# Other places, queues and steps for partial sums, x and head outputs in a hybrid attention layer on one core

## The chip, the cores and the metric

The kernel runs on one core of a Trainium2 chip. The metric is the device time of one execution in microseconds; lower is better. The runs shown of the kernel before took 2504.91, 2508.32 and 2502.14 us, median 2504.91.

## What is computed

One decoder layer over 1024 tokens of width 2048, all in float32. x is normalised and multiplied by a weight matrix of 2048 x 8192; the columns are q, k, v and gate of 8 stick-breaking heads and of 8 differential heads (partial rotary on q and k of the latter). Cut to what matters:

```python
hn = rmsnorm(h, norm_mix_g)
sb_q, sb_k, sb_v, sb_g, df_q, df_k, df_v, df_g = split(hn @ w_in)
sb_out = stick_breaking_attention(sb_q, sb_k, sb_v)        # w = sigmoid(z) * prod of (1 - sigmoid)
df_out = rmsnorm(differential_attention(df_q, df_k, df_v, lam), subln_g)
mixed = concat([sb_out * silu(sb_g), df_out * silu(df_g)])
h = h + mixed @ w_out
h = h + sigmoid(rmsnorm(h, norm_ple_g) @ w_ple_gate) * (p @ w_ple_proj)
return rmsnorm(h, norm_final_g)
```

## The kernel before, in words

Everything is kept transposed: features on 128 partitions, tokens along the free axis, in two halves of 512 tokens with the order of the tokens reversed. "Half 1" is worked on first and "half 0" second (for brevity: the first half and the second half of the attention stage). Every float32 operand is split into a rounded part and a rest (hi and lo, fp32r), and a product of two operands is three matmuls: hi x hi, lo x hi, hi x lo (L219 to L221 in `unit`, L517 to L519 in `Seven.product`). ScalarE (ACT) makes the hi part, VectorE (DVE) the lo part.

The order of the work: (1) v and gate of the stick-breaking heads for both halves by a seven-product scheme of 2 x 2 blocks (class `Seven`, instance `gv`, L645 to L943); its results go to the DRAM tile `vg_d`. (2) Attention: for each half, heads 8 to 15 (differential), then 0 to 7 (stick-breaking), L957 to L1060. A differential head has two units of projection, a stick-breaking one has one; a unit is 32 groups of three matmuls. (3) The output projection, again with `Seven` (instance `op`, L1175 to L1357), (4) gate, embedding and final norm.

**Filler and side steps.** TensorE's order is written out by hand (`manual_schedule`). While TensorE does a unit, the attention of the head before is woven in: `attention` returns a list of (slot, function), `Side.add` sorts it behind the current slot, and `Side.tick` is called after each group of three matmuls in `unit` (and in `Seven.product` where `tick` is set) and runs what is due. So a "slot" is one group of three matmuls. Of each head there are `weights` (scores for one block of 128 query rows; matmuls L289 to L298), `values` (transposition of v, L343), and for two pairs of row blocks `turn` (transposition of weights, L359, then hi and lo, L368 to L376) and `mix` (weights times v, L391 to L396; after the last one the sum is read by ACT L401 and DVE L402), and for differential heads `norm` (L422, L423). `SECOND` and `LATD` set when the second pair starts, `tight` marks head 15. The PSUM tiles av, tp, vps, msq and ssps share the tag "t" with two buffers.

**The other queues.** Outside the stretches marked `man2`, VectorE and ScalarE are ordered by a scheduler ahead of the run, as SyncE's (SP) and GpSimd's (POOL) DMA queues are everywhere: it takes what it holds ready, in the order of the program. Each engine then works strictly in that order. SP issues weights (L153, L532, L562), x (L663, L716, L965), operands (L1184) and the stores of L1219; POOL issues the stores of L743 and L698, the loads of vf and gf (L984), of k and v, and the accumulating stores into `comb_d` (L254 to L265).

**First sums.** In both uses of `Seven` the first eight units (phase 0) start with a filler: for each pair of units the product "A11" is made, copied to a tile s1 (tag "sq", two buffers) and stored (`vgpart_d`, L743, or `part_d`, L1219), then "A12" is added and the sum goes out through a tile of the ring "f" (four buffers, `ftile`). After the filler, for each unit, s1 is loaded again (L885, L1298) and added to the product "S2" (L893, L1306) before the product "S1" follows.

**x of the second half.** For half 0 each of 16 blocks of x is loaded into a tile "xt" (four buffers, L965) and split into xh and xl by `split_scaled` (L139, L140). The tiles xh and xl of a block are the ones that the first half used, so they are free when TensorE has read them for the last time. The DRAM tile `h_d`, to which the output projection is added later, gets its copy of x in half 0 (L1060) and, for eight blocks, earlier (L930).

Of the kernel before, what the change touches and what calls it, by code (L numbers as in the profile page):

```python
# [17 lines left out]
ALU = mybir.AluOpType  # L18
# [30 lines left out]
def _body(ctx, nc, tc, ap):  # L49
# [218 lines left out]
    def attention(at, pz, half, hd, q, qz, K, KL, VV, sg, vf):  # L268
# [188 lines left out]
    with tc.tile_pool(name="at", bufs=2) as at, tc.tile_pool(name="pz", bufs=2, space=PSUM) as pz:  # L457
# [23 lines left out]
        class Seven:  # L481

            def __init__(self, w, n):
                self.w = w
                self.units = [(ph, u) for ph in range(2) for u in range(n)]
                self.wq, self.XC, self.T = {}, {}, {}
                self.made, self.late, self.slot = [], 0, 0
                self.raws = []
                self.xq = deque()
                self.after = None  # L490
# [32 lines left out]
            def first(self, u, parts=((slice(0, 2), slice(0, 4 * P)),), between=None):  # L523

                raw = wp.tile([P, 2, 4 * P], F32, name="wraw", tag="wraw", bufs=2)
                self.raws.append(raw)
                hi = wp.tile([P, 2, 4 * P], F32R, name="wfh", tag="whi")
                lo = wp.tile([P, 2, 4 * P], F32R, name="wfl", tag="wlo")
                for k, f in parts:
                    if isinstance(k, slice):  # L530
                        for j in range(2):
                            nc.sync.dma_start(raw[:, j, f], self.w(u, 0, j)[:, 0, f])  # L532
                    else:
                        nc.sync.dma_start(raw[:, k, f], self.w(u, 0, k)[:, 0, f])
                    if between:
                        between(k, f)

                def cast(k, f):
# [3 lines left out]
                for i, nm in enumerate(("A11", "A12")):  # L542
                    self.wq[u, 0, nm] = hi[:, i], lo[:, i]
                if between:
                    return cast
                for k, f in parts:
                    cast(k, f)
# [153 lines left out]
        cast0 = gv.first(0, parts[:2], xloads)  # L701
        cast1 = gv.first(1, parts1, lambda k, f: None)
        for i in range(4):
            load1(1, i)
            if i == 1:
                nc.sync.dma_start(gv.raws[0][:, 1, :], gv.w(0, 0, 1)[:, 0, :])
                nc.sync.dma_start(gv.raws[1][:, 1, :], gv.w(1, 0, 1)[:, 0, :])
# [20 lines left out]
        nslot = 0  # L728
# [6 lines left out]
        for u in range(0, H, 2):  # L735
            aa = [pp.tile([P, HALF], F32, name="pa", tag="acc", bufs=2) for _ in range(2)]
            for i in range(2):
                gv.product(u + i, 0, "A11", aa[i], True)
                s1 = ev.tile([P, HALF], F32, name="s1", tag="sq", bufs=2)
# [4 lines left out]
                if u:  # L744
                    some(4)
            for i in range(2):
# [4 lines left out]
                if u < H - 2:  # L751
                    gv.first(u + 2 + i)
# [117 lines left out]
        for ph in range(2):  # L870
            for u in range(H):
# [5 lines left out]
                s1 = ev.tile([P, HALF], F32, name="s1", tag="sq", bufs=2)  # L877
# [6 lines left out]
                else:  # L884
# [72 lines left out]
        for half in (1, 0):  # L957
# [4 lines left out]
            else:  # L962
                for kt in KT:
                    xt = ev.tile([P, HALF], F32, name="xt", tag="xt", bufs=4)
                    nc.sync.dma_start(xt, ap["xT"][kt * P:(kt + 1) * P, tsl])  # L965
                    X[kt] = split_scaled(kt, xt, gvec[:, 0, kt:kt + 1])
# [3 lines left out]
            for hd in (ORDER0, ORDER1)[half]:  # L970
# [9 lines left out]
                acc = unit(X)  # L980
                if sb:
                    vf, gf = f32t("vf"), f32t("gf")
                    for i, t in enumerate((vf, gf)):
                        G.dma_start(t, vg_d[half, i, hd])  # L984
# [40 lines left out]
                if sb:  # L1025
                    vacc = vf, gf
# [254 lines left out]
        for ph in range(2):  # L1281
            for u in range(8):
# [7 lines left out]
                s1 = ev.tile([P, HALF], F32, name="s1", tag="sq", bufs=2)  # L1290
# [6 lines left out]
                else:  # L1297
# [251 lines left out]
```

## Time and profile before

| what | value |
|---|---|
| median of the runs shown | 2504.91 us |
| the profiled execution's own time | 2504.86 us |
| its span, first to last instruction | 2503.1 us |
| mean granted TensorE clock | 0.989 |
| DMA, mean over the span | 161 GB/s |

In a table of stretches each row gives the stretch in us from the start of the span and its length, then the busy time with the count of instructions for TensorE (PE), its weight loads (PEld), VectorE, ScalarE and GpSimd, then the granted TensorE clock, the busy share of the DMA engines and GB/s. In a timeline each row gives start and duration in us, engine, line, operation, output<-inputs, shapes and count; in brackets stands how long the engine sat idle before it and what ended that. Where the engine named had been done for long, another wait ended last. A "q" behind an engine's name is its queue.

### The profile page before, as it was taken

What the parts mean: (1) busy time and instruction counts of PE and PEld (TensorE: products, weight loads), DVE (VectorE), ACT (ScalarE), POOL (GpSimd) and SP (SyncE); (2) the same over time, 40 slices, a digit from 0 to 9 for tenths busy, and PEclk for the clock granted to TensorE, in tenths of its full rate; (3) what the DMA queues carried; (4) which work ended last, traced back from release to release, by engine and by line L of the source; (5) the groups of instructions that cost most, each with busy time, mean ns of one, the idle gap of its engine ahead of it and who ended that gap; (6) DMA issues with size and microseconds to landing.
All of it is one profiled execution on the core that took longest, in us unless ns stands there. A gap on an engine that the chain in (4) does not pass through costs nothing.

```text
span 2503.1 us, 31940 instructions
## 1 busy us (share of the span) xinstructions
PE 2419.8 (97%) x11434; PEld 2007.0 (80%) x11434; DVE 1793.0 (72%) x3010; ACT 1216.1 (49%) x2066; POOL 297.5 (12%) x393
## 2 busy tenths in 40 slices
PE   8999999999999999999999989999899999999997
PEld 6787878888888887888888877887787887787886
DVE  6888776777777777778888877778578664546555
ACT  6243345555565445555656664445423224546443
POOL 1211110000010010000000001110111112330110
PEclk9999999999999999999999999999999999999998
DMA  8777654434344555444444434545746777343333
GB/s 287 265 261 225 213 185 137 153 118 135 121 143 152 164 170 179 128 125 122 125 128 116 125 110 118 144 126 177 244 160 215 169 189 230 119 133 103 130 110 102
DMA packets 165424, 397.72 MB, mean 159 GB/s; under 512 B 18896, under 2 KB 23248, under 8 KB 165264
## 3 DMA queue, kind: packets, MB, share of 16 engines
q1 hardware_dynamic: 126432, 293.68, 36.6%
q0 software_dynamic: 38832, 102.00, 15.4%
q8 instruction: 90, 1.47, 0.2%
q14 instruction: 70, 0.57, 0.1%
HBM read 297.03 MB, written 106.95 MB: 161 GB/s over the span
## 4 chain that ended last, share of the span: by engine, by line
PE 78%; DVE 8%; issue 7%; DMA 3%; ACT 3%; POOL 1%; SPq 0%; DVEq 0%; POOLq 0%; ACTq 0%
PE acc L219 16%; PE acc L220 16%; PE acc L221 16%; PE pbc L517 3%; PE pbc L519 3%; PE pbc L518 3%; PE tp L359 2%; DVE st L320 1%; PE av L396 1%; PE z L297 1%; PE z L298 1%; PE pa L517 1%; PE pa L519 1%; PE pa L518 1%; PE av L394 1%
## 5 line engine op out<-in xcount | busy, mean ns | idle before, releaser
L219 PE MATMUL acc<-xh,whi 128*128 128x512 f32 x1568 | 629.8, 402 | 1.5 <-DVE gt L1166 1.5
L221 PE MATMUL acc<-xh,wlo 128*128 128x512 f32 x1568 | 614.5, 392 | 0.0
L220 PE MATMUL acc<-xl,whi 128*128 128x512 f32 x1568 | 614.3, 392 | 0.0
L150 DVE TENSOR_TENSOR wlo<-wraw,whi 128x1024 fp32r<-128x1024 f32 x252 | 312.5, 1240 | 240.9 <-ACT whi L149 235.5
L149 ACT CAST whi<-wraw 128x1024 fp32r<-128x1024 f32 x252 | 264.9, 1051 | 290.0 <-PE acc L220 260.2
L221 PEld LDWEIGHTS acc<-xh,wlo 128*128 128x128 f32 x1568 | 295.8, 189 | 64.8 <-DVE wlo L150 0.2
L219 PEld LDWEIGHTS acc<-xh,whi 128*128 128x128 f32 x1568 | 296.3, 189 | 57.2 <-issue 2.4
L220 PEld LDWEIGHTS acc<-xl,whi 128*128 128x128 f32 x1568 | 296.7, 189 | 54.8 <-issue 0.5
L608 ACT CAST wpr<-T 128x512 fp32r<-128x512 f32 x128 | 78.0, 621 | 317.3 <-DVE T L566 313.0
L375 ACT CAST awh<-tp 128x256 fp32r<-128x256 f32 (+1 forms) x160 | 80.1, 501 | 160.0 <-PE tp L359 128.1
L376 DVE TENSOR_TENSOR awl<-tp,awh 128x256 fp32r<-128x256 f32 (+1 forms) x160 | 92.8, 580 | 62.4 <-ACT awh L375 60.8
L111 POOL TENSOR_TENSOR ssq<-ssq,sq 128x512 f32<-128x512 f32 x56 | 83.8, 1498 | 304.5 <-ACT sq L110 253.8
L328 ACT ACTIVATE et<-z,mx 128x512 f32<-128x512 f32 (+7 forms) x128 | 94.4, 738 | 50.9 <-DVE mx L325 50.0
L320 DVE TENSOR_TENSOR_SCAN st<-pt 128x511 f32<-128x511 f32 (+3 forms) x64 | 86.5, 1352 | 20.5 <-ACT pt L318 20.5
L325 DVE TENSOR_REDUCE mx<-z 128x1 f32<-128x512 f32 (+7 forms) x128 | 96.2, 752 | 1.2
L517 PE MATMUL pbc<-cS,wpr 128*128 128x512 f32 x224 | 88.4, 395 | 7.4 <-DVE u L1306 5.8
L622 DVE TENSOR_TENSOR wpr<-T,wpr 128x512 fp32r<-128x512 f32 x128 | 87.6, 684 | 6.3 <-ACT wpr L608 4.5
L396 PE MATMUL av<-awl,v 128*128 128x256 f32 x256 | 76.0, 297 | 12.6 <-DVE awl L376 12.5
L518 PE MATMUL pbc<-cS,wpr 128*128 128x512 f32 x224 | 88.1, 393 | 0.0
L519 PE MATMUL pbc<-cS,wpr 128*128 128x512 f32 x224 | 87.9, 392 | 0.0
L394 PE MATMUL av<-awh,v 128*128 128x256 f32 x256 | 73.0, 285 | 5.2 <-ACT awh L375 5.2
L219 PE MATMUL acc<-cA11h,whi 128*128 128x512 f32 x192 | 76.0, 396 | 0.0
(401 smaller groups left out, 5341.2 us busy)
## 6 DMA issues: line engine op xcount, KB each, us to landing
wraw<-w_in SPq DMA_DIRECT2D x192, 512.0 KB, 3.6
wraw<-w_gate SPq DMA_DIRECT2D x64, 512.0 KB, 3.6
wraw<-w_out SPq DMA_DIRECT2D x72, 256.0 KB, 3.6
wraw<-w_vg SPq DMA_DIRECT2D x71, 256.0 KB, 4.0
comb_d<-sg POOLq DMA_DIRECT2D x48, 256.0 KB, 7.4
spare<-xT SPq DMA_DIRECT2D x44, 256.0 KB, 4.0
vghalf_d<-hc POOLq DMA_DIRECT2D x32, 256.0 KB, 4.3
h_d<-xT SPq DMA_DIRECT2D x32, 256.0 KB, 6.2
```

Of the source, the lines that this page charges most:

```text
L149: A.copy(hi[:, o], raw[:, o])
L150: V.tensor_tensor(lo[:, o], raw[:, o], hi[:, o].bitcast(F32), op=ALU.subtract)
L219: T.matmul(acc[c], hi[:, k2, kh, c, :], xh, start=first, stop=False)
L220: T.matmul(acc[c], hi[:, k2, kh, c, :], xl, start=False, stop=False)
L221: T.matmul(acc[c], lo[:, k2, kh, c, :], xh, start=False, stop=last)
L320: V.tensor_tensor_scan(st[:, off + 1:nkey], pt[:, off:nkey - 1], pt[:, off:nkey - 1], initial=1.0, op0=ALU.mult, op1=ALU.bypass)
L325: V.reduce_max(mx, z[:, vw], axis=AX.X, negate=True)
L394: T.matmul(av, vv[:, 0, blk % 4, :], wh, start=blk == 2 * pr + 1, stop=False)
L396: T.matmul(av, vv[:, 0, blk % 4, :], wl, start=False, stop=last)
L517: T.matmul(o, wh[:, w], xh, start=start and k == 0, stop=False, skip_group_check=True)
L518: T.matmul(o, wh[:, w], xl, start=False, stop=False, skip_group_check=True)
L519: T.matmul(o, wl[:, w], xh, start=False, stop=k == 3, skip_group_check=True)
```

## The change

It has these parts:

- **Steps.** Head 0 starts its scores at slot 12 instead of 10; head 15's second pair starts 13 slots behind its last scores instead of 8; the last `mix` of the second pair of every stick-breaking head comes two slots later.
- **vf and gf** of a stick-breaking head are loaded at the third quarter of its unit (`mid={2: load_vg}`) from SP's queue, not after the unit from POOL's.
- **x of the second half** is loaded from `h_d[0]` straight into the memory of xl, and split in place. For this, `h_d[0]` is filled in half 1 (two blocks a head, heads 8 to 15) and `h_d[1]` in half 0.
- **First sums** use tiles of the ring "f"; the first two (units 0 and 1) are loaded again during the filler, into the tag "sq", and phase 0 takes them from there.
- **The start.** `first` is divided into `load` (DMA) and a cast; the weights of units 2 and on are ordered after the product "A11" instead of after "A12", and the x tiles `raw2[1]` to `raw2[3]` are ordered behind them.

```diff
@@ attention
-            b = 10 if hd == 0 else 6
+            b = 12 if hd == 0 else 6
             ss, t0 = [[b], [b + 3], [b + 7], [b + 11]], b + 16
...
-            t1 = s3[-1] + (8 if tight else LATD[half])
+            t1 = s3[-1] + (13 if tight else LATD[half])
...
-            steps.append((t + gap * n, partial(mix, pr, n - 1)))
+            steps.append((t + gap * n + (2 if sb and pr else 0), partial(mix, pr, n - 1)))
@@ class Seven
-            def first(self, u, parts=((slice(0, 2), slice(0, 4 * P)),), between=None):
+            def load(self, u, parts=((0, slice(0, 4 * P)), (1, slice(0, 4 * P))), between=None):
...
+                def fetch(k, f):
+                    nc.sync.dma_start(raw[:, k, f], self.w(u, 0, k)[:, 0, f])
+
                 for k, f in parts:
...
+                    fetch(k, f)
                     if between:
                         between(k, f)
...
+                return cast, fetch
+
+            def first(self, u):
+                self.load(u)[0]()
@@ gv, ahead of the filler
-        for i in range(4):
+
+        def load2(i):
             for c in range(2):
                 nc.sync.dma_start(raw2[i][c], xsrc(0, KX[0][i][c]))
+
+        load2(0)
@@ gv, the filler
-                s1 = ev.tile([P, HALF], F32, name="s1", tag="sq", bufs=2)
+                s1 = ftile()
                 if u == 0:
                     some(3)
                 A.copy(s1, aa[i])
                 G.dma_start(vgpart_d[u + i], s1)
-                if u:
+                if u + 2 + i < H:
+                    casts[u + 2 + i] = gv.load(u + 2 + i)[0]
+                else:
+                    s1s[i] = ev.tile([P, HALF], F32, name="s1", tag="sq", bufs=2)
+                    nc.sync.dma_start(s1s[i], vgpart_d[i])
+                if u == 0:
+                    load2(1 + i)
+                    if i:
+                        load2(3)
+                else:
                     some(4)
...
                 if u < H - 2:
-                    gv.first(u + 2 + i)
+                    casts.pop(u + 2 + i)()
@@ phase 0, and the same in op with part_d
-                s1 = ev.tile([P, HALF], F32, name="s1", tag="sq", bufs=2)
+                early = ph == 0 and u in s1s
+                s1 = s1s.pop(u) if early else ev.tile([P, HALF], F32, name="s1", tag="sq", bufs=2)
...
-                else:
+                elif not early:
                     nc.sync.dma_start(s1, vgpart_d[u])
@@ half 0
-                    xt = ev.tile([P, HALF], F32, name="xt", tag="xt", bufs=4)
-                    nc.sync.dma_start(xt, ap["xT"][kt * P:(kt + 1) * P, tsl])
-                    X[kt] = split_scaled(kt, xt, gvec[:, 0, kt:kt + 1])
+                    hi = xp.tile([P, HALF], F32R, name=f"xh{kt}", tag=f"xh{kt}")
+                    lo = xp.tile([P, HALF], F32R, name=f"xl{kt}", tag=f"xl{kt}")
+                    nc.sync.dma_start(lo.bitcast(F32), h_d[0, kt])
+                    A.activation(hi, lo.bitcast(F32), AF.Copy, scale=gcol(kt))
+                    V.scalar_tensor_tensor(lo, lo.bitcast(F32), gcol(kt), hi.bitcast(F32), op0=ALU.mult, op1=ALU.subtract)
+                    X[kt] = hi, lo
...
-                acc = unit(X)
-                if sb:
-                    vf, gf = f32t("vf"), f32t("gf")
-                    for i, t in enumerate((vf, gf)):
-                        G.dma_start(t, vg_d[half, i, hd])
+                def load_vg():
+                    for i in range(2):
+                        vg.append(f32t(("vf", "gf")[i]))
+                        nc.sync.dma_start(vg[i], vg_d[half, i, hd])
+
+                vg = []
+                acc = unit(X, mid={2: load_vg} if sb else None)
...
-                if half == 0 and hd >= H:
+                if hd >= H:
                     for kt in (2 * (hd - H), 2 * (hd - H) + 1):
-                        for hf in range(1 if kt in KT[8:] else 2):
-                            with tc.issue_after(lastw[0].ins):
-                                nc.sync.dma_start(h_d[hf, kt], ap["xT"][kt * P:(kt + 1) * P, hf * HALF:hf * HALF + HALF])
+                        if half == 0 and kt in KT[8:]:
+                            continue
+                        with tc.issue_after(lastw[0].ins):
+                            nc.sync.dma_start(h_d[1 - half, kt], xsrc(1 - half, kt))
@@ op, the filler
-                s1 = ev.tile([P, HALF], F32, name="s1", tag="sq", bufs=2)
+                s1 = ftile()
                 A.copy(s1, aa[i])
                 nc.sync.dma_start(part_d[u + i], s1)
+                if u == 4:
+                    s1s[i] = ev.tile([P, HALF], F32, name="s1", tag="sq", bufs=2)
+                    nc.sync.dma_start(s1s[i], part_d[i])
```

More of the change, by code (lines that the diff above doesn't have):

```diff
@@ L487, in __init__ @@
                 self.made, self.late, self.slot = [], 0, 0
-                self.raws = []
                 self.xq = deque()
@@ L700, in _body @@
         A.preload_act_table_set("natural_log_exp_and_others")
-        cast0 = gv.first(0, parts[:2], xloads)
-        cast1 = gv.first(1, parts1, lambda k, f: None)
+        cast0, fetch0 = gv.load(0, parts[:2], xloads)
+        cast1, fetch1 = gv.load(1, parts1)
         for i in range(4):
@@ L705, in _body @@
             if i == 1:
-                nc.sync.dma_start(gv.raws[0][:, 1, :], gv.w(0, 0, 1)[:, 0, :])
-                nc.sync.dma_start(gv.raws[1][:, 1, :], gv.w(1, 0, 1)[:, 0, :])
+                fetch0(*parts[2])
+                fetch1(*parts[2])
         for k in range(2):
@@ L727, in _body @@
         todo.extend(partial(divide, "S3", i) for i in range(4))
-        nslot = 0
+        casts, s1s = {}, {}
         def some(n):
@@ L883, in _body @@
                         rest_of(prev, True)
-                else:
+                elif not early:
                     nc.sync.dma_start(s1, vgpart_d[u])
@@ L1025, in _body @@
                 if sb:
-                    vacc = vf, gf
+                    vf, gf = vacc = vg
                 else:
@@ L1289, in _body @@
                     nc.sync.dma_start(r[e], half_d[e])
-                s1 = ev.tile([P, HALF], F32, name="s1", tag="sq", bufs=2)
+                early = ph == 0 and u in s1s
+                s1 = s1s.pop(u) if early else ev.tile([P, HALF], F32, name="s1", tag="sq", bufs=2)
                 if ph:
@@ L1296, in _body @@
                         rest_of(prev, True)
-                else:
+                elif not early:
                     nc.sync.dma_start(s1, part_d[u])
```

15 lines of the change are left out of this document (3 added, 12 removed).

## Prediction

> **What bounds the kernel now.** I read the profiled execution first: it took 2504.86 us, 1.8 us more than its span, and the runs shown have the median 2504.91 us, so a saving in the span is taken from 2504.9 without a correction. Then the page's engine row, the table of stretches, and the timeline around each stretch in which TensorE (PE) was idle.
>
> ```profile
> span 2503.1 us, 31940 instructions
> PE 2419.8 (97%) x11434; PEld 2007.0 (80%) x11434; DVE 1793.0 (72%) x3010; ACT 1216.1 (49%) x2066; POOL 297.5 (12%) x393
> 600.00:650.00 50.00, 50.00 (x241) 41.86 (x240) 38.33 (x85) 28.33 (x57) 2.65 (x4) 1.00 0.39 121
> 940.00:965.00 25.00, 20.51 (x90) 16.51 (x89) 20.49 (x35) 16.99 (x31) 0.55 (x1) 0.86 0.74 235
> 1425.00:1480.00 55.00, 49.21 (x243) 41.02 (x242) 40.55 (x76) 35.98 (x59) 4.87 (x7) 0.94 0.38 106
> 1510.00:1545.00 35.00, 31.48 (x152) 25.91 (x151) 25.26 (x34) 16.18 (x25) 4.30 (x6) 0.90 0.39 103
> 1798.00:1820.00 22.00, 16.23 (x62) 12.94 (x61) 12.62 (x20) 7.71 (x15) 1.68 (x3) 0.84 0.74 240
> ```
>
> The reader is to see that PE is the bound (97%) and that in a quiet stretch (600 to 650) it has no idle time at all, with VectorE busy for 38.33 of 50 us and ScalarE for 28.33. No work is removed from PE here: the change can only close the 83.3 us in which PE idles, and the matmuls that run slowly beside such gaps. Four stretches in the table hold much of it: their PE columns miss 4.5, 5.8, 3.5 and 5.8 us, and their granted clock is 0.84 to 0.94 instead of 1.00.
>
> How a gap costs twice is seen at 1470, in PE's timeline:
>
> ```profile
> 1470.25 0.47 PE L359 MATMUL tp<-ident,et 128*128 128x128 f32 x1 [4.25 <-DVE et L336]
> ...
> 1470.95 0.63 PE L220 MATMUL acc<-xl,whi 128*128 128x512 f32 x1
> 1471.38 0.63 PE L221 MATMUL acc<-xh,wlo 128*128 128x512 f32 x1
> ...
> 1475.65 0.45 PE L293 MATMUL z<-k,q 128*128 128x512 f32 x1
> 1476.40 0.39 PE L219 MATMUL acc<-xh,whi 128*128 128x512 f32 x1
> 1476.63 0.39 PE L220 MATMUL acc<-xl,whi 128*128 128x512 f32 x1
> ```
>
> After 4.25 us of idling, starts are 0.43 us apart instead of 0.23 from 1470.95 to 1475.65: 11 steps, 2.2 us lost besides the gap. A side slot of the schedule (three matmuls) is 3 x 0.23 = 0.69 us at full clock.
>
> [...]
>
> **Part 1: later steps where head types change.** Head 15 (differential) is followed by head 0 (stick-breaking). The gap at 1470.25 is the first transposition of head 15's second pair, placed 8 slots behind its last scores and waiting for the weights of L336. Five slots later (13) PE gets there 5 x 0.69 = 3.4 us later, with matmuls of the projection in between: 4.25 - 3.4 = 0.8 us stays, I take 1.1 because the L336 chain itself may slip, and the slow clock (2.2) goes. **Gain 5.3 us.** Head 0's own steps go two slots back (10 to 12), which keeps its scores behind that transposition.
>
> The last mix of a stick-breaking pair 1 comes two slots later. It pays at the end of the first half:
>
> ```profile
> 997.44 0.50 PE L391 MATMUL av<-lead,v 128*128 128x256 f32 x2 [1.52 <-DVE lead L369]
> ```
>
> Two slots are 1.4 us of cover for this 1.52 us: **gain 1.3.** In the second half, though, the last mix of such a head isn't late; there another mix of the pair waits, once for each of heads 1 to 4:
>
> ```profile
> 1637.26 0.39 PE L396 MATMUL av<-awl,v 128*128 128x256 f32 x1 [1.09 <-DVE awl L376]
> ...
> 1642.56 0.28 PE L396 MATMUL av<-awl,v 128*128 128x256 f32 x1
> 1643.34 0.55 DVE L402 TENSOR_REDUCE sm<-av 128x128 f32<-128x384 f32 x1
> ```
>
> The 1.09 us before L396 (second mix, VectorE busy with a scan) isn't touched. The last mix (1642.56) gives its PSUM tile free when L402 ends at 1643.9, 1.05 us after it. The tag "t" has two buffers for av, tp, vps and msq alike. Moved by two slots, that release is due at 1645.3, and the next head's first transposition asks for a buffer 1.7 us behind the mix (vps 0.35 and two slots). So it just fits; the bounds are nothing and, if the mix's reader queues behind a scan so that the vps buffer must serve, the hold of a vps less 1.7:
>
> ```profile
> 1493.21 0.60 PE L343 MATMUL vps<-ident,vf 128*128 128x128 f32 x4
> 1496.85 0.55 PE L359 MATMUL tp<-ident,bt 128*128 128x128 f32 x3 [1.41 <-DVE v L346]
> ```
>
> The transposition of 1496.85 waited for the reader of vps, so that tile held its buffer for 3.6 us from 1493.21: at most 1.9 per head. I take 0.2 (near the L402 row), seven heads: **loss 1.4.** Between heads 0 and 1 it is worse. Head 0 starts two slots later, so its last transposition (slot 84, counted from head 15's registration) falls on the same slot as head 1's vps, and its last mix (90) behind head 1's first transposition (86). Three tiles want two buffers. The trace shows two slots between such steps:
>
> ```profile
> 1532.11 0.60 PE L359 MATMUL tp<-ident,bt 128*128 128x128 f32 x4
> 1534.17 0.65 PE L343 MATMUL vps<-ident,vf 128*128 128x128 f32 x4
> ```
>
> The vps at 1534.17 came just when tp from 1532.11 was read, 1.7 us after tp's transpositions; with no slots between, PE waits those 1.7 us. Then slot 86 meets a vps that may be held for 3.6 us after 1.7 us of work: up to 1.9, taken as 1.1, and slot 90 meets the 1.05 us of L402 less one mix of 0.7: 0.6 with its queue. **Loss 3.4**; bounds 0.5 and 5.5 (both with slow matmuls). The wait of 1.41 us at 1496.85 has the same cause (msq of head 15 in slot 58 beside vps); the norm now falls in slot 63, one slot ahead of the next transposition, so I count **0.2** there.
>
> **Part 2: vf and gf from SP in mid-unit instead of from POOL behind it.** The gap at 1522 is a queue's doing:
>
> ```profile
> 1502.07 0.88 POOL L260 DMA_DIRECT2D comb_d<-sg  x1 [9.91 <-DVE q L1005]
> ...
> 1503.73 1.60 POOL L984 DMA_DIRECT2D vf<-vg_d  x1
> 1512.16 0.69 DVE L1030 TENSOR_TENSOR vf<-vf,ssa 128x512 f32<-128x512 f32 x1 [4.85 <-DMA vf<-vg_d]
> 1522.52 0.51 PE L391 MATMUL av<-lead,v 128*128 128x256 f32 x2 [2.52 <-DVE lead L369]
> ...
> 1524.18 0.58 PE L396 MATMUL av<-awl,v 128*128 128x256 f32 x1 [0.76 <-DVE awl L376]
> ```
>
> Head 1's vf load stood on POOL's queue behind three accumulating stores of head 15 (from 1502.07), landed 8.4 us after its issue at 1503.73, and VectorE stood 4.85 us at L1030 with scans and lead queued behind it; PE paid 2.52 and 0.76 us, and some nine slow steps at +0.20 us as after 1470 (1.8; clock 0.90 in the table). At pc = 2 the load is issued 16 slots, 11 us or more, earlier, and no longer behind those stores; vf of the head before holds one of four buffers "f", the other three are free by then. It now stands on SP's queue between weight loads: two issues of about 0.33 us (SP issued two in 0.94 us at 15.65) and 0.5 MB a head. If the first had to wait for a buffer, the weights behind it would wait too, and with them PE after the 8 slots (5.5 us) that one piece of weights lasts; in 600 to 650 that queue leaves the DMA engines 61% idle, so nothing is taken. With 4.85 us back, VectorE is ahead of the lead: I take 0.5 left, **gain 4.6**. Elsewhere in the stick-breaking heads PE doesn't wait for vf: nothing.
>
> **Part 3: x of the second half straight into xl.**
>
> ```profile
> 946.51 7.19 SPq L965 DMA_DIRECT2D xt<-xT  x5
> 951.85 0.72 ACT L139 ACTIVATE xh<-xt,gvec 128x512 fp32r<-128x512 f32 x1 [2.59 <-DMA xt<-xT]
> 954.43 0.58 PE L394 MATMUL av<-awh,v 128*128 128x256 f32 x1 [3.70 <-ACT awh L375]
> ```
>
> ScalarE waits 2.59 us for an xt that came through a ring of four buffers (the first of the five issued from 946.51 on landed 5.3 us later); the head's awh is queued behind it and PE idles 3.70 us. The table misses 4.5 us of PE in that stretch, and its clock of 0.86 stands for some ten slow steps (2 us, as after 1470): 6.5 us. Without xt, a load starts when PE has read xl for the last time, four per quarter of a unit, and nothing waits for VectorE to empty xt. The same bytes move, and ACT's and VectorE's instructions stay 16 each. But ScalarE's order is fixed beforehand, so a load that lands later than planned still blocks awh: bounds 0 and 6.5 left, taken 1.5, since each group of four has a whole unit (32 slots, 22 us) before PE needs it. **Gain 5.0.** Of the 24 copies into h_d in the second half, 8 stay and 16 go to the first half, two a head, on SP's queue behind a weight load. There the DMA share is 0.39 (600 to 650) and PE has no gap: nothing; without that cover, a weight load held up by one copy could come later by a landing, 5.3 us.
>
> **Part 4: first sums return early.** At the start of the output projection's second stage:
>
> ```profile
> 1799.71 0.46 SPq L1298 DMA_DIRECT2D s<-part_d  x1
> DMA to landing us min/median/max: 8.2/8.2/8.2
> 1802.75 1.29 DVE L506 TENSOR_TENSOR cA<-cA 128x512 fp32r<-128x512 f32 x2 [0.66 <-ACT cA L505]
> 1808.07 0.69 DVE L1306 TENSOR_TENSOR u<-pbc,s 128x512 f32<-128x512 f32 x1 [4.03 <-DMA half_d<-hc]
> 1808.91 0.77 PE L517 MATMUL pbc<-cS,wpr 128*128 128x512 f32 x1 [5.77 <-DVE u L1306]
> 1810.74 0.69 DVE L566 TENSOR_TENSOR T<-wraw 128x512 f32<-128x512 f32 x1 [1.98 <-DMA wraw<-w_out]
> 1813.97 0.68 DVE L622 TENSOR_TENSOR wpr<-T,wpr 128x512 fp32r<-128x512 f32 x1
> ```
>
> The row at 1808.07 names a store, but the tile s that L1306 reads was ordered at 1799.71 and took 8.2 us: it landed at 1807.9. PE's next product waits for L1306. With s there since unit 4, L1306 follows L506 at 1804.04 and PE starts at 1804.9, not 1808.9: 4.0 us, and 1.8 of slow steps. But then S1 and S3 (24 x 0.23 = 5.5) end at 1810.3, and unit 1's S2 needs weights whose raw block only lands at 1810.7 (L566 at 1810.74, low part until 1814.65). One load of 262 kB less ahead of it is 1.1 us at the stretch's 240 GB/s. So S2 of unit 1 can be finished some 3 us earlier than now, less half a microsecond of slow matmuls. **Gain 2.5**, bounds 0 and 5.8. In the value stage s is no wait, since VectorE comes to its L893 with no idle time before it:
>
> ```profile
> 65.22 0.68 DVE L893 TENSOR_TENSOR u<-pbc,s 128x512 f32<-128x512 f32 x1
> ```
>
> The sums now use the ring "f": four tiles a pair of units, 4 x 12 x 0.23 = 11 us of matmuls until a slot returns, longer than the 8.2 us of the slow landing above: nothing; if a store took 11 us, PE would wait by the excess.
>
> **Part 5: the order at the start.**
>
> ```profile
> 14.91 0.33 SPq L559 DMA_DIRECT2D b<-w_vg  x1
> 15.65 0.94 SPq L532 DMA_DIRECT2D wraw<-w_vg  x2
> 23.91 0.50 PE L517 MATMUL pa<-cA11h,wfh 128*128 128x512 f32 x1 [1.81 <-ACT wfh L539]
> ```
>
> PE waits 1.81 us for weights ordered at 15.65. They are now written ahead of six x loads, but the scheduler issues what is ready: at 14.91 it had already taken a block that is written far later, so the weights weren't ready before. I take 0 of a possible 4 (1.81 and slow steps as after 1470).
>
> **Sum:** 5.3 + 1.3 - 1.4 - 3.4 + 0.2 + 4.6 + 5.0 + 2.5 = 14.1. Forecast 2504.9 - 14.1 = **2490.8 us**.
>
> **Rivals.** *The waits move* (0.17): buffers "t" cost 5.5 between heads 0 and 1 and 0.5 at seven heads, x still blocks ScalarE (gain 1.5) and the weights take all of part 4: 5.3 + 1.3 - 3.5 - 5.5 + 0.2 + 4.6 + 1.5 = 3.9, so 2501. For it: tags shared by four tiles. Against: the fit at 1643.9. *More than the sum* (0.17): freed from vf, VectorE's order also turns in heads 1 to 4 (4 x 1.09), the start gives 4 and parts 3 and 4 another 4: 14.1 + 4.4 + 4 + 4 = 26.5, so 2478. *The early orders don't come early* (0.05), since slots or in-order waits hold them: only part 1 (2.0) and half of part 2 (2.3) are left: 2501. *Slower* (0.08), one mechanism: x can no longer be fetched ahead of PE's last read, and ScalarE stands for each of the four groups. If three of them stall PE as the one at 954 does (6.5 each), 19.5 replaces 6.5; the other gains are 9.1, so it decides from 15.6 us lost in 930 to 990. With four groups and the first unit of head 8 starved too, 5 x 6.5 = 32.5 in place of 6.5, less 9.1: 17 slower, 2522. Against: landings of 5 us against 22 us of lead.
>
> **Numbers.** My forecast 0.53, own range 2484 to 2497. A difference under 0.3% (7.5 us) is about what a measurement can't tell from none. Faster by more: 0.51 + 0.17 + 0.05 + 0.02 = 0.75; slower 0.05; within 0.20. Two in ten are left out by 2477 to 2503.
>
> **What would show it.** No idle of 4 us before L359 near 1466, no L1030 wait for vf, no ACT wait for xt near 950, L1306 without a wait. New waits should stand before L343 and L359 between heads 0 and 1, and for wraw after 1805. If gaps near 940 to 965 grow, or vps waits recur per head, the prediction is wrong.

## The result, and the profile after

The change makes the kernel slower. Its median is 2515.72 us (2511.86 to 2517.95, six runs), beside 2505.51 for the kernel before: ratio 1.0038, 95% interval 1.0023 to 1.0052, some 10 us. The profiled execution took 2515.73 us. From the page and the table of stretches of the changed kernel:

```profile
PE 2421.5 (96%) x11434; PEld 2005.8 (80%) x11434; DVE 1792.6 (71%) x3010; ACT 1215.5 (48%) x2067; POOL 279.6 (11%) x361
```

```profile
1425.00:1480.00 55.00, 54.04 (x274) 45.00 (x273) 42.15 (x77) 38.47 (x61) 3.78 (x5) 1.00 0.38 107
1480.00:1510.00 30.00, 23.05 (x109) 18.68 (x108) 23.24 (x34) 14.65 (x23) 3.69 (x5) 0.89 0.40 118
1510.00:1545.00 35.00, 28.44 (x144) 23.74 (x144) 21.74 (x28) 15.45 (x24) 0.59 (x3) 0.95 0.28 65
```

and one row of the kernel before, for a stretch that the prediction didn't show:

```profile
1480.00:1510.00 30.00, 27.27 (x147) 23.03 (x146) 22.27 (x33) 15.93 (x25) 4.91 (x7) 1.00 0.48 124
```

TensorE does the same 11434 matmuls. In 1425 to 1480 it now works 54.04 us, 4.8 more than before: the idle of 4.25 us at 1470 is gone, as forecast. But in the next stretch it works 23.05 of 30 us instead of 27.27, and in 1510 to 1545, where a gain of 4.6 us was expected, 28.44 of 35 instead of 31.48, with 144 matmuls instead of 152. So waits have moved by one stretch. (From 1510 on the kernel is 3 us late and more, so a stretch holds slightly earlier work.)

The new waits of 1480 to 1510, in TensorE's, ScalarE's and VectorE's timelines of the changed kernel:

```profile
1485.48 0.39 PE L396 MATMUL av<-awl,v 128*128 128x256 f32 x1 [1.71 <-DVE awl L376]
...
1498.08 0.29 PE L422 MATMUL msq<-sqh,onesr 128*128 128x256 f32 x1
...
1499.47 1.28 ACT L91 ACT_TABLE_LOAD   x1
...
1501.76 1.28 ACT L92 ACT_TABLE_LOAD   x1
...
1503.50 0.43 DVE L93 SCALAR_TENSOR_TENSOR sqv<-msq,rsub 128x256 f32<-128x256 f32 x1 [1.03 <-ACT rsub L92]
...
1503.98 1.12 PE L359 MATMUL tp<-ident,bt 128*128 128x128 f32 x4 [3.45 <-DVE sqv L93]
```

The norm of head 15 (slot 63 now) makes msq at 1498.08. Its last reader, L93, starts at 1503.50, behind two table loads of ScalarE. Head 0's first mix has taken the other buffer of the tag "t" in the meantime, so the transposition waits 3.45 us. Ahead of it the mixes of head 15's moved second pair stand 1.29 us before awh (1483.27) and 1.71 us before awl (1485.48), where the kernel before has 0.76 us: a part of what the later transposition saved at 1470 is paid here.

The waits behind them, in POOL's, ScalarE's and TensorE's timelines:

```profile
1508.58 1.45 POOL L265 DMA_DIRECT2D comb_d<-sg  x1
...
1516.03 1.28 ACT L1050 ACT_TABLE_LOAD   x1 [5.42 <-DMA comb_d<-sg]
1517.33 0.63 ACT L1050 ACTIVATE sg<-gf 128x512 f32<-128x512 f32 x1
...
1521.26 0.39 PE L394 MATMUL av<-awh,v 128*128 128x256 f32 x1 [2.00 <-ACT awh L375]
...
1524.10 0.57 PE L396 MATMUL av<-awl,v 128*128 128x256 f32 x1 [2.34 <-DVE awl L376]
```

ScalarE stands 5.42 us at the sigmoid of head 2 until the last accumulating store of head 15 has landed; awh and awl behind it are late and TensorE idles 2.00 and 2.34 us. The stores start at 1507.38 (1502.07 in the kernel before), in part because the norm ahead of them comes five slots later: with the steps alone (e1 below) they start at 1504.11.

Then the x blocks and the first sums, in ScalarE's and TensorE's timelines:

```profile
955.29 0.50 PE L391 MATMUL av<-lead,v 128*128 128x256 f32 x2 [1.81 <-DVE lead L369]
...
956.08 0.72 ACT L978 ACTIVATE xh<-xl,gvec 128x512 fp32r<-128x512 f32 x1 [2.40 <-DMA xl<-h_d]
...
957.11 0.38 PE L394 MATMUL av<-awh,v 128*128 128x256 f32 x1 [1.32 <-ACT awh L375]
...
1813.94 0.47 PE L516 MATMUL pbc<-cS,wpr 128*128 128x512 f32 x1 [1.60 <-DVE u L1327]
...
1822.36 0.50 PE L516 MATMUL pbc<-cS2h,wpr 128*128 128x512 f32 x1 [2.73 <-ACT wpr L606]
...
1824.21 0.55 PE L518 MATMUL pbc<-cS2h,wpr 128*128 128x512 f32 x1 [1.12 <-DVE wpr L620]
```

The wait for xt (2.59 us before) is now one of 2.40 us for xl, and the idle of 3.70 us at 954 is 1.81 and 1.32. The 5.77 us before the product behind u became 1.60, followed by 2.73 and 1.12 for weights.

### The profile page after: what moved, and what is told of

It is laid out like the page before. It is cut to its first block, busy times and chain, and to the rows that moved or that the text cites. A ratio compares the mean times of both kernels' runs of the same rounds, so it can differ in the third digit from the quotient of the medians.

```text
span 2514.0 us, 31908 instructions
## 1 busy us (share of the span) xinstructions
PE 2421.5 (96%) x11434; PEld 2005.8 (80%) x11434; DVE 1792.6 (71%) x3010; ACT 1215.5 (48%) x2067; POOL 279.6 (11%) x361
## 4 chain that ended last, share of the span: by engine, by line
PE 79%; DVE 10%; DMA 5%; ACT 4%; issue 3%; SPq 0%; DVEq 0%; POOL 0%; ACTq 0%
PE acc L219 16%; PE acc L220 16%; PE acc L221 16%; PE pbc L518 4%; PE pbc L516 4%; PE pbc L517 4%; PE tp L359 2%; DVE st L320 2%; PE pa L518 1%; PE pa L516 1%; PE pa L517 1%; PE av L396 1%; PE z L297 1%; PE z L298 1%; PE av L395 1%
## 5 line engine op out<-in xcount | busy, mean ns | idle before, releaser
L375 ACT CAST awh<-tp 128x256 fp32r<-128x256 f32 (+1 forms) x160 | 80.1, 501 | 150.2 <-PE tp L359 124.8
L318 ACT ACTIVATE pt<-z 128x512 f32<-128x512 f32 (+3 forms) x64 | 41.6, 651 | 81.6 <-DVE z L304 80.4
```

## The experiments

Each run stands beside runs of the kernel before on the same chip; what is compared is the ratio to those. A ratio of 1.0010 is 2.5 us. The theories at the start: **S**, the changed steps carry the slowdown, for most of the new waits stand at them; **Q**, the moved loads do.

**e1_steps_alone.** The three step lines of the diff and nothing else:

```diff
+            b = 12 if hd == 0 else 6
+            t1 = s3[-1] + (13 if tight else LATD[half])
+            steps.append((t + gap * n + (2 if sb and pr else 0), partial(mix, pr, n - 1)))
```

> The kernel before with nothing but the three changed steps (head 0 at slot 12, the second pair of head 15 13 slots behind its scores, the last mix of a stick-breaking second pair two slots later). Theory S (the steps carry the slowdown, through the two-buffer PSUM tag t and the later norm of head 15): the idle of 4.25 us before L359 at 1470 is gone, but a wait of 3 to 4 us stands before the transposition behind head 15's norm, 2 us before L343 two heads later, and each later stick-breaking head is about 0.4 us longer; the kernel is 4 to 10 us slower than before. Theory Q (the moved loads carry it): the steps are worth what the prediction gave them, some 2 us, and the kernel is 0 to 4 us faster than before.

Measured 2503.87 us, ratio 0.9997 (0.9989 to 1.0006): theory S falls. The waits that it named are there (3.45 us before L359, 2.23 before L343 at 1530), and yet nothing is lost, because the steps also cure the stretch behind them, with 175 matmuls in 35 us where the kernel before does 152 and no idle time of 2.52 us before lead:

```profile
1510.00:1545.00 35.00, 31.71 (x175) 26.83 (x174) 26.27 (x36) 16.99 (x27) 4.92 (x7) 1.00 0.42 109
```

POOL's and ScalarE's timelines show how:

```profile
1491.81 0.54 POOL L984 DMA_DIRECT2D vf<-vg_d  x1 [1.58 <-PE vps L343]
...
1504.11 0.91 POOL L260 DMA_DIRECT2D comb_d<-sg  x1 [7.50 <-DVE sg L426]
...
1510.33 1.03 ACT L318 ACTIVATE pt<-z 128x1024 f32<-128x1024 f32 x1 [1.20 <-DVE z L304]
...
1512.19 0.63 ACT L1034 ACTIVATE sg<-gf 128x512 f32<-128x512 f32 x1
```

With the norm and its stores later, POOL's order has vf ahead of the stores, twelve microseconds earlier than before (1503.73) and still on its old queue. And ScalarE's order has the sigmoid (L1034) behind the next scores' pt, at 1512.19, where it waits for nothing. So part 1 alone did what part 2 was meant to do, and the prediction counted that gain once, in part 2.

**e2_steps_undone.** The opposite cut, on the changed kernel:

```diff
-            b = 12 if hd == 0 else 6
+            b = 10 if hd == 0 else 6
-            t1 = s3[-1] + (13 if tight else LATD[half])
+            t1 = s3[-1] + (8 if tight else LATD[half])
-            steps.append((t + gap * n + (2 if sb and pr else 0), partial(mix, pr, n - 1)))
+            steps.append((t + gap * n, partial(mix, pr, n - 1)))
```

> The changed kernel with the three steps put back to 10, 8 and no delay; all moved loads stay. Theory S: the waits before L359 near 1500 and before L343 near 1538 are gone, the 4.25 us at 1470 are back; x and vf gain something, so the time is 1 to 8 us under before (2497 to 2504). Theory Q: the time stays at 2511 or more, near the changed kernel's.

Measured 2511.53 us, ratio 1.0031 (1.0020 to 1.0042). Theory Q: the moved loads and sums cost some 8 us.

**e3_mix_undone.** The changed kernel with only the delay of the last mix taken out:

```diff
-            steps.append((t + gap * n + (2 if sb and pr else 0), partial(mix, pr, n - 1)))
+            steps.append((t + gap * n, partial(mix, pr, n - 1)))
```

> The changed kernel with only the two-slot delay of the last mix undone. If the delay costs what the changed trace suggests (0.45 us in each of seven stick-breaking heads of the second half, 2.2 and 0.5 us before L343 and L359 between heads 0 and 1, as many heads again in the first half at a part of that), the time falls by 4 to 7 us against the changed kernel, less 1.3 us at the end of the first half. If the delay is harmless, the time stays within 2 us of the changed kernel.

Measured 2518.15 us, ratio 1.0053 (1.0040 to 1.0066): not faster but, if anything, slower than the changed kernel; the expectation was wrong. TensorE's waits in the first half's last heads, first in e3, then in the changed kernel (us in total, times, longest):

```profile
PE av L394 <- ACT awh L375: 2.8, 1, 2.8
PE av L396 <- DVE awl L376: 2.7, 8, 0.7
PE av L391 <- DVE lead L369: 2.4, 2, 1.8
```

```profile
PE av L396 <- DVE awl L376: 2.5, 4, 1.2
PE av L391 <- DVE lead L369: 1.8, 1, 1.8
PE av L394 <- ACT awh L375: 1.3, 1, 1.3
PE z L294 <- DVE k L1021: 1.1, 1, 1.1
```

Without the delay 2.8 + 2.7 + 2.4 = 7.9 us, with it 2.5 + 1.8 + 1.3 + 1.1 = 6.7. It costs in the second half (a wait that the kernel before doesn't have, from the same view of 1545 to 1730),

```profile
PE tp L359 <- DVE sm L402: 2.5, 6, 1.2
```

and saves somewhat more in the first: from 790 to 1005 TensorE does 998 matmuls in e3 and 1022 in the changed kernel, from 1545 to 1770 it does 1131 and 1112. e8 uses that.

**e4_sg_later.** The changed kernel, the sigmoid that stood at 1516 ordered behind its own head's k (`lastk` is the last copy of L1020):

```diff
-                    lastsig[0] = A.activation(sg, gf, AF.Sigmoid)
+                    with tc.issue_after(lastk.ins) if half == 0 and hd == 2 else __import__("contextlib").nullcontext(): lastsig[0] = A.activation(sg, gf, AF.Sigmoid)
```

> The changed kernel; ScalarE's sigmoid of head 2 in the second half (L1050, which stood 5.4 us until the accumulating stores of head 15 had landed and given the third sg tile free) is ordered behind the same head's k. Nothing else on TensorE moves. If this second wait is what ate the gain of the early vf: the idle of 2.00 and 2.34 us before awh and awl near 1520 goes, with the slow matmuls beside it, and the time falls by 4 to 6 us. Rival: head 15's scans and the lead would have been late anyway, and the time falls by 1 us or less.

Measured 2510.65 us, ratio 1.0024 (1.0014 to 1.0033) where the changed kernel has 1.0038: some 3.5 us less by the ratios, 5 by the medians, and 4 to 6 expected. The stretch runs at full clock:

```profile
1510.00:1545.00 35.00, 32.20 (x177) 27.14 (x177) 23.67 (x32) 16.24 (x25) 4.58 (x6) 1.00 0.40 102
```

**e5_x_alone, e6_vg_alone, e7_sums_alone.** Each group of the moved loads by itself on the kernel before: x into xl with the copies into `h_d`; vf and gf from SP; the first sums with the new start.

```diff
@@ e5_x_alone
+                    nc.sync.dma_start(lo.bitcast(F32), h_d[0, kt])
@@ e6_vg_alone
+                acc = unit(X, mid={2: load_vg} if sb else None)
@@ e7_sums_alone
+                s1 = ftile()
...
+                early = ph == 0 and u in s1s
```

> The kernel before with only the x of the second half loaded from h_d straight into the memory of xl (and the copies into h_d moved for it). As the prediction had it: the idle of 3.70 us before awh at 954 shrinks to about 1 us and the time falls by 3 to 5 us. By what the changed kernel with its steps undone shows (2.4 us lost between 892 and 988, an idle of 3.28 us before awh still there): the time is 1 to 4 us above before.

> The kernel before with only vf and gf of the stick-breaking heads loaded from SP's queue at the third quarter of the unit. As the prediction had it: no wait of 4.85 us at vf, 2.52 us before lead at 1522 goes to 0.5, time 3 to 5 us less. Theory of a second wait: ScalarE's sigmoid of head 2 still waits until the stores of head 15 have landed, so the idle near 1522 stays at 2 to 4 us and nothing is gained there; and with the products of vf and gf elsewhere in VectorE's order, each stick-breaking head is 0.3 to 0.6 us longer; the time is 3 to 7 us above before.

> The kernel before with only the first sums through the ring f and back early, and the new order of the loads at the start. As the prediction had it: the 5.77 us at 1803 shrink to about 2 us, with waits for weights behind, 0 to 5 us less. By what the other kernels' traces show: 0.8 us lost by 40 us, 0.9 by 64 and 0.8 by 182, and of the gap at 1803 no more than 1 us gained in the sum, since two waits for weights (2 and 1.1 us) take its place: 1 to 4 us above before.

Measured: x 2505.57 us, ratio 1.0009 (1.0000 to 1.0017); vf and gf 2506.79 us, 1.0016 (1.0008 to 1.0025); sums and start 2505.47 us, 1.0005 (0.9997 to 1.0014). Their sum, 1.0030, is e2's 1.0031. With the steps (0.9997) it is 1.0027, within the interval of the whole change. No gain of any of the three arrived.

In x alone, ScalarE and TensorE:

```profile
952.19 0.72 ACT L967 ACTIVATE xh<-xl,gvec 128x512 fp32r<-128x512 f32 x1 [2.44 <-DMA xl<-h_d]
952.82 0.25 ACT L368 CAST lead<-tp 128x128 fp32r<-128x128 f32 x1
...
953.95 0.50 PE L391 MATMUL av<-lead,v 128*128 128x256 f32 x2 [2.77 <-DVE lead L369]
```

ScalarE stands 2.44 us for the first block of the third group, which was ordered at 947.02, when TensorE had read its place for the last time, and landed 5.2 us later. In the kernel before the lead stood ahead of that wait, now it stands behind it: 2.77 us idle before L391. With vf and gf alone:

```profile
1513.93 1.28 ACT L1036 ACT_TABLE_LOAD   x1 [5.42 <-DMA comb_d<-sg]
...
1526.06 0.79 PE L391 MATMUL av<-lead,v 128*128 128x256 f32 x2 [3.95 <-DVE lead L369]
```

vf came early, and the sigmoid waited 5.42 us for the stores: 3.95 us idle before lead instead of 2.52. ScalarE's order has changed, too: the cast of awh that stood ahead of this sigmoid in the kernel before (1509.90) now stands behind it (1515.76). The larger part of the loss lies elsewhere, in the stick-breaking heads of the first half. First the kernel before, then e6:

```profile
725.00:920.00 195.00, 194.31 (x959) 161.88 (x959) 142.18 (x267) 98.52 (x195) 17.10 (x28) 1.00 0.53 161
```

```profile
725.00:920.00 195.00, 191.96 (x942) 159.64 (x941) 140.72 (x264) 97.11 (x191) 10.03 (x15) 1.00 0.51 159
```

TensorE works 2.3 us less there. In the seven traces with early vf and gf it works 190.7 to 192.0 us in this stretch, in the eight without 193.5 to 194.3, so the loss belongs to this part. In e6 the waits are 1.2 us before L297 and 0.6 before L391 between 720 and 805 (0.5 and none in the kernel before), then a quarter of a microsecond before awl in each of four heads from 800 to 925. Which change in VectorE's or ScalarE's order makes them isn't shown.

**e13_vg_sg_later.** e6 with the two edits of e4 (`lastk`, and the sigmoid behind it), and nothing else.

> The kernel with vf and gf from SP alone (e6_vg_alone), and ScalarE's sigmoid of head 2 behind the same head's k. If the wait for head 15's stores was all that held the early vf back: the idle of 3.95 us before lead at 1522 goes, 4 to 6 us less than e6_vg_alone, 0 to 2 us under before (the 0.5 us in each stick-breaking head of the first half stay). Rival: VectorE's order keeps the lead late by itself; within 2 us of e6_vg_alone, 2 to 4 above before.

Measured 2505.49 us, ratio 0.9998 (0.9989 to 1.0007), some 4.5 us under e6. The idle before lead is 0.44 us:

```profile
1522.99 0.50 PE L391 MATMUL av<-lead,v 128*128 128x256 f32 x2 [0.44 <-DVE lead L369]
```

That is the 0.5 us that the prediction wrote down, and it needed the second wait gone: TensorE now works 33.57 us at clock 1.00 from 1510 to 1545, instead of 31.48 at 0.90. But from 725 to 920 it works 191.95 us, as in e6. So what the early loads gain at 1522 is lost again in the first half.

**e9_x_late.** e5 with ScalarE's third group behind the awh (L375) made last:

```diff
+                    with tc.issue_after(lastwh[0].ins) if kt in KT[8:12] else __import__("contextlib").nullcontext(): A.activation(hi, lo.bitcast(F32), AF.Copy, scale=gcol(kt))
```

> The kernel with the x of the second half alone (e5_x_alone), and ScalarE's part of its third group of four blocks ordered behind the last awh of the head that is being mixed; the loads stay where they are. If what eats the gain of this part is ScalarE's fixed order (it stands 2.4 us for a block that lands 5.2 us after TensorE has given its place free, with lead and awh queued behind it): the idle of 2.77 us before lead and 1.10 us before awh near 953 goes, with the slow matmuls beside it, and the time is 4 to 6 us under e5_x_alone's, 2 to 4 under before. Rival: the groups that follow run into the next head's q and k instead; 1 us or nothing.

Measured 2501.84 us, ratio 0.9990 (0.9981 to 0.9999), 5 us better than e5. The lead goes first and all four blocks follow without a wait; the idle before L391 is 1.35 us:

```profile
950.37 0.28 ACT L368 CAST lead<-tp 128x128 fp32r<-128x128 f32 x1
...
952.02 0.50 PE L391 MATMUL av<-lead,v 128*128 128x256 f32 x2 [1.35 <-DVE lead L369]
...
955.64 2.56 ACT L967 ACTIVATE xh<-xl,gvec 128x512 fp32r<-128x512 f32 x4
...
967.12 0.51 PE L391 MATMUL av<-lead,v 128*128 128x256 f32 x2 [1.69 <-DVE lead L369]
```

The last row is the rival's share: the next head's lead is late by 1.69 us, where e5 has 1.03 and the kernel before none. The profiled execution of e9 took 2505.20 us, 3.4 more than the median, so its trace shows the order, not the size of the gain.

**e12_sums_out.** The early sums in the output projection alone, on the kernel before:

```diff
+                s1 = ftile()
                 A.copy(s1, aa[i])
                 nc.sync.dma_start(part_d[u + i], s1)
+                if u == 4:
+                    s1s[i] = ev.tile([P, HALF], F32, name="s1", tag="sq", bufs=2)
+                    nc.sync.dma_start(s1s[i], part_d[i])
...
+                early = ph == 0 and u in s1s
```

> The kernel before with the early return of the first sums in the output projection only; the value stage and the order of the loads at the start stay as before. If the 3.4 us that the trace of e7_sums_alone gains around 1805 are this part's and the rest of that kernel (start and value stage) takes them back: 2 to 3 us under before, about 4 us under e7_sums_alone. Rival: the waits for weights behind it take the gain here too; within 1 us of before.

Measured 2503.95 us, ratio 0.9996 (0.9988 to 1.0005):

```profile
1804.86 0.47 PE L517 MATMUL pbc<-cS,wpr 128*128 128x512 f32 x1 [1.60 <-DVE u L1310]
...
1812.15 0.50 PE L517 MATMUL pbc<-cS2h,wpr 128*128 128x512 f32 x1 [1.60 <-ACT wpr L608]
...
1814.00 0.80 PE L519 MATMUL pbc<-cS2h,wpr 128*128 128x512 f32 x1 [1.12 <-DVE wpr L622]
```

5.77 us became 1.60 + 1.60 + 1.12 = 4.32. The product starts at 1804.86, where the prediction had 1804.9; the rest of the wait was a wait for weights, and what is left of the gain can't be told from none. Between e12 and e7 lie 2 us with overlapping intervals: whether the start costs something stays open.

**e8_msq_copied.** The steps of e1 on the kernel before, with the delay in the first half only, and msq copied out of PSUM at once for head 15:

```diff
+            steps.append((t + gap * n + (2 if sb and pr and half == 1 else 0), partial(mix, pr, n - 1)))
...
+            if hd == 2 * H - 1 and pr == 1: ps, msq = msq, ev.tile([P, 2 * P], F32, name="msc", tag="sm", bufs=5); V.tensor_copy(msq, ps)
             rs_ = ev.tile([P, 2 * P], F32, name="rsub", tag="sm", bufs=5)
```

> The kernel before with the changed steps, but the two-slot delay of the last mix in the first half only, and the norm of head 15's second pair copied out of PSUM by VectorE as soon as TensorE has made it, so that its buffer of the tag t comes free before ScalarE's two table loads and not behind them. If that hold is what costs the 3.5 us before the transposition near 1500 and the delay costs 0.4 us a head in the second half: 5 to 8 us less than the steps alone, 2496 to 2499. If the next tile on the two buffers takes the wait over: 2 us less or nothing.

Measured 2498.65 us, ratio 0.9981 (0.9973 to 0.9990): about 4 us under e1 by the ratios, a little less than expected. The copy and the undone delay were not run apart, so how the 4 us divide is not shown. The copy takes 0.41 us, and the transposition doesn't wait:

```profile
1496.51 0.41 DVE L424 COPY msc<-msq 128x256 f32<-128x256 f32 x1
...
1497.33 0.60 PE L359 MATMUL tp<-ident,bt 128*128 128x128 f32 x4
...
1525.72 0.66 PE L343 MATMUL vps<-ident,vf 128*128 128x128 f32 x4 [2.05 <-DVE awl L376]
```

The last row, 2.05 us before vps, is the prediction's wait of 1.7 us at slot 84 with three tiles on two buffers; it stays.

**e10_mended, e11_best.** e10 is the changed kernel with the lines marked + in e4, e8 and e9 (the delay in the first half only, msq copied, the sigmoid and the third x group later). e11 is e8 with x as in e9 and the sums as in e12; vf and gf stay on POOL.

> The changed kernel with all its parts and four repairs: the norm of head 15 copied out of PSUM at once, the two-slot delay in the first half only, the sigmoid of head 2 behind its own k, the third x group behind the awh. If the waits found so far are the whole cause, the repairs add up (about 5, 2, 5 and 4 us): 2499 to 2503, 2 to 6 us under before. If the moved loads cost something that no repair touches (0.5 us in each stick-breaking head of the first half): 2504 to 2508.

> e8_msq_copied (changed steps with the delay in the first half only, norm copied out of PSUM; 2498.7 us) with two parts of the change added: x of the second half straight into xl with the third group ordered behind the awh, and the early return of the first sums in the output projection only. vf and gf stay on POOL's queue and the start is as before. If the parts add up: 3 to 5 us from x and 2 to 3 us from the sums, 2490 to 2494. Rival (they compete for the same stretch or give back later): 2496 to 2499.

Measured: e10 2500.12 us, ratio 0.9986 (0.9977 to 0.9995), where the changed kernel has 1.0038: some 13 us less (15.6 by the medians), as expected if the repairs add up. So the repaired waits are more than the whole of the slowdown, though the loss from 725 to 920 stays (191.43 us). e11 2495.99 us, ratio 0.9968 (0.9956 to 0.9979), faster than both kernels. It came out 2 us short of its expectation, at the edge of its rival's, and its interval overlaps that of e8, so what x and the sums add there is not clear of the noise.

## Why the prediction was wrong

The forecast was 14.1 us less; it is some 10 more. Run alone, the parts give 0.8 gained and 4.0, 2.3 and 1.3 lost (e1, e6, e5, e7), together 6.7 lost; the rest is within the intervals.

- **Part 1, right in sum, by luck.** Net gain 2.0 forecast, 0.8 measured (e1, interval -1.5 to 2.8). But the terms were off both ways. The gap at 1470 went (0.82 us left in e1 where 1.1 was taken; 4.8 more TensorE time in 1425 to 1480 of the changed kernel), though a wait of 1.66 us came behind it, at 1483 in e1. The step "the norm now falls in slot 63, one slot ahead of the next transposition" (0.2) failed: it cost a wait of 3.45 us. The rows of the kernel before had said so:

```profile
1495.04 0.28 PE L422 MATMUL msq<-sqh,onesr 128*128 128x256 f32 x1
...
1498.91 0.42 DVE L93 SCALAR_TENSOR_TENSOR sqv<-msq,rsub 128x256 f32<-128x256 f32 x1 [1.39 <-ACT rsub L92]
...
1499.99 0.40 PE L391 MATMUL av<-lead,v 128*128 128x256 f32 x2
```

msq was held there from 1495.04 to 1499.3, and head 0's av took its buffer just behind that. Moved five slots, msq starts one slot ahead of av, and the third tile waits. Set against it was a gain not forecast here, the cure of the stall near 1522. The 1.7 us for vps came as 2.23 (e1). The delay of the last mix costs more in the second half than the 0.2 us a head forecast (2.5 us in six waits in the changed kernel) and, beside the moved loads, saves somewhat more than that in the first (e3).
- **Part 2, two steps that failed.** The first: "With 4.85 us back, VectorE is ahead of the lead." Two waits ended together in the kernel before, and I took away the one that ended last by 0.7 us. The other was in its profile, in ScalarE's timeline:

```profile
1511.46 1.28 ACT L1034 ACT_TABLE_LOAD   x1 [0.98 <-DMA comb_d<-sg]
```

It also needs a correction: the vf load at 1503.73 isn't head 1's but that of head 2, fetched one unit ahead. Its sg tile is the fourth of a ring of three, behind those of heads 15, 0 and 1, so it waits until head 15's stores have landed. In e6 the sigmoid stood ahead of an awh as well, and nothing was gained there (30.36 us of TensorE's work from 1510 to 1545, 31.48 before). The second: "Elsewhere in the stick-breaking heads PE doesn't wait for vf: nothing." The early loads took 2.3 us of TensorE's work from the first half (194.31 to 191.96 us in 725 to 920). Gain 4.6 forecast, 4.0 lost (e6); with the sigmoid moved, 0.5 gained (e13), within the error of none, since the gain at 1522 arrived and the first half took it back.
- **Part 3:** the step that took 1.5 of 6.5 us as left failed, though its bound named the mechanism, that a late landing blocks awh in ScalarE's fixed order. The likeliest value had to lie near that bound: the lead of 22 us was TensorE's need, not the place that the order gives ScalarE. Gain 5.0 forecast, 2.3 lost (e5); put behind the awh, 2.5 gained (e9).
- **Part 4:** 2.5 forecast, 1.0 measured for the output projection alone (e12, interval -1.3 to 3.0): the weights behind it took most of the gain, as the bound of 0 had it.
- **Part 5:** nothing forecast, and nothing found: the wait of 1.81 us for weights at the start is 1.69 in the changed kernel and 2.35 in e8, which has the old start, so such differences aren't the change's.

Of the rivals, "the waits move" named the right kind of thing, but gave it no loss; "slower" named ScalarE standing for x and asked for three such groups at 6.5 us each; one group stood, the part lost 2.3 us, and the larger loss came from vf and gf.

## What to carry to other kernels

Ahead of crediting a wait that is taken away, list every wait that ends within a few microseconds of it on the engines behind it: here the next one took its place (e6: 3.95 us idle before the lead where the kernel before has 2.52). Where an engine's order is fixed ahead of the run, an earlier load helps only as far as the order places its consumer (e5: lead stood behind a wait of 2.44 us for x); look for which instruction stands behind the consumer, and look at every head in which the load moves, not only at the one that waited. A step that is moved takes its hold on a buffer along (msq: 3.45 us before the transposition), so lay the hold, not the instruction, beside its new neighbours.

## What the runs showed of the hardware

An idle of about 2 us was followed by a lower clock in e8 and by full clock in e1 and e4. In e8, after the 2.05 us at 1525.72 above, with no gap over 0.4 us in the 7 us before it, the table of stretches has:

```profile
1525.00:1530.00 5.00, 4.28 (x16) 3.49 (x17) 2.38 (x5) 0.97 (x3) 0.00 (x0) 0.69 0.00 0
```

The granted clock is 0.69, and starts are 0.43 us apart from about 1527 to 1530. The same wait is 2.23 us in e1 (L343, at 1530) and 2.07 us in e4 (1534.19), and there the clock of 1510 to 1545 stays at 1.00 (rows above). In e12 an idle of 1.60 us (1804.86) is followed by a clock of 1.00, too.

The traces of the two kernels show more of this. Up to 20 us before the end they have 16 stretches at clock 0.50, seven in the kernel before and nine in the changed one. Each lasts 3.41 or 6.83 us, and within a trace they begin whole multiples of 3.41 us apart, so I cut both traces into windows of 3.41 us from those beginnings. In the window just ahead of each of the 16, TensorE was idle for 49 to 100%. Of the windows at full clock with full clock behind them, one in each trace was idle for more than half (56% from 2274.47 in the kernel before, 55% from 2285.32 in the changed kernel), all others for 47% or less. So in these two traces the length of a gap alone did not tell what followed. In the kernel before, the 1.81 us at 23.91 fall into the window from 21.67, which is idle for 66%, and clock 0.50 follows from 25.08 to 28.49; the 1.81 us at 2070.60 are divided between the windows from 2066.25 and 2069.67, idle for 26 and 27%, and the clock stays at 1.00. How the waits of e8, e1, e4 and e12 lie to such windows is not shown.

Ln and Exp of one norm (L91 and L92), with only a copy between them, cost two table loads of 1.28 us each in the changed kernel (rows at 1499.47 and 1501.76). The sigmoid's activation starts 0.02 us after its load (1516.03 + 1.28 = 1517.31, then 1517.33), and the second load of the norm starts 0.02 us after the copy ahead of it (1501.13 + 0.61 = 1501.74, then 1501.76).
